# One core of Trainium2: a hybrid pooling, convolution and stick-breaking attention block whose input is normed with tokens on partitions and transposed by TensorE, its projections leaving PSUM unscaled

## The chip, the cores and the metric

The kernel runs on one core of one Trainium2 chip. The metric is the device time in microseconds (us) of one execution, as the median of several runs. The engines are TensorE (PE; its weight loads are listed apart as PEld), VectorE (DVE), ScalarE (ACT), GpSimd (POOL) and SyncE (SP), which here only issues transfers. Each runs its own instructions in order, and instructions on different engines wait for each other through semaphores.

## What is computed

One layer over 1024 tokens of width 1024, all in float32, cut to what matters here:

```
h = x * rsqrt(mean(x*x, -1) + 1e-6) * g_pre                 # pre-norm
u = h @ w_in                       # ten groups of 512 columns, then 3*1024 merge logits
y_pool = pool_mixer(pool_v) * silu(pool_g)
y_conv = gate_b * (causal_conv3(gate_c * conv_x) + bias) * silu(conv_g)
y_sb   = stick_breaking_attention(q, k, v) * silu(sb_g)     # 8 heads of 64
merged = sum over branches of sigmoid(merge_b) * (y_b @ w_branch_b)
out    = x + rms_norm(merged @ w_out, g_post)
```

The norm's factor `rsqrt(...)` belongs to a token, so it may be applied before the projection or after it.

## The kernel before

Everything is held with channels on the partitions and tokens along the free dimension, in two halves of 512 tokens (`HALVES`, t = 0 and 1). Each float32 operand is split into a high part (a cast to float32r) and a low part (operand minus high part), and each product is three matmuls: high by high, high by low, low by high. So one block of 128 output channels of the input projection takes, for each token half, 8 slices of the contraction by 3 matmuls, 24 in all (`half_block`, L136); `block` (L146) runs both halves and hands each PSUM bank to a function `post`.

The host gives x twice: as it is, for the residual at the end, and transposed (`x_t`), with channels on partitions. At the start (L178 to L228) `x_t` comes in seven transfers, in pieces of one to four slices; each slice is multiplied by its channel's `g_pre` and split by ACT (`hh`, L198) and DVE (`hl`, L199), and TensorE takes each slice as it comes. The sum of squares over channels runs beside that: POOL squares (L212, the last four on ACT, L214), DVE adds up (L216), TensorE sums over the partitions (`ssq`, L220), POOL takes the power -0.5 (L133), TensorE spreads the factor over the partitions (`bc`, L224), and DVE copies it to `rstd_bc` (L225). Every projection is then multiplied by `rstd_bc` as it leaves PSUM (`scale_into`, L160 to L163), on DVE.

The first two projected blocks (keys and queries of the first head pair, weights `first_w` and `second_w`) are computed in this start. Then come 64 steps of attention (L395 to L425), one for each head and block of 128 queries: logits `z` (L349, L350) on TensorE, two sigmoids on ACT, a scan on DVE (L354), a product and a mask on POOL (L356, L114), transposes `tp` on TensorE (L373), their split on ACT and DVE (L374, L252), and products `o` with the values (L387). Between these steps TensorE is given projections as filler (`fillers`, L324). A scheduler sets the final order on each engine from the data dependences; the source order is only its start. After the attention come the gates and the branches (`merge_first`, `pool_branch`, `merge_next`, `conv_branch`, `merge_last`) and the output projection with the post-norm.

Weights come through SP's queue in 256 KB pieces, three buffers deep (`next_w`, L82), and are split by ACT (L79) and POOL or DVE (L80).

Of the kernel before, what the change touches and what calls it, by code (L numbers as in the profile page):

```python
# [34 lines left out]
def hybrid_block_kernel(ctx, tc, x, x_t, g_pre, w_in, pool_w, pool_scale, conv_w, conv_b, w_branch, w_out, g_post, out):  # L35
# [16 lines left out]
    bigp = op("big", 2 * KB)  # L52

    def h_tiles(name):
        return [[bigp.tile([P, 2, HALF], F32R, tag="big", name=f"{name}{t}_{i}") for i in range(KB // 2)] for t in range(2)]
# [40 lines left out]
    gpre_sb = const.tile([P, KB], F32, name="gpre_sb")  # L96
    nc.scalar.dma_start(gpre_sb, g_pre)
# [13 lines left out]
    rstd_bc = const.tile([P, S], F32, name="rstd_bc")  # L111
# [17 lines left out]
    def rstd_from(ssq, n, pool):  # L129
        var = pool.tile([P, n], F32, tag="var", name="var")  # L130
        nc.vector.tensor_scalar(out=var, in0=ssq, scalar1=1.0 / D, scalar2=EPS, op0=ALU.mult, op1=ALU.add)
        r = pool.tile([P, n], F32, tag="rstd", name="rstd")
        nc.gpsimd.tensor_tensor(out=r, in0=var, in1=expo[:, 0:n], op=ALU.pow)  # L133
        return r

    def half_block(ps, ws, t):  # L136
        n = 0
        for k in range(KB):
            hi, lo = ws[k // 4]
            a = slice(k % 4 * P, (k % 4 + 1) * P)  # L140
# [37 lines left out]
    with tc.tile_pool(name="xp", bufs=2 * KB) as xp, tc.tile_pool(name="ps_s", bufs=1, space=PSUM) as ps_s:  # L178
        xts, first_w, second_w = [], [], []
        for t, k0, k1 in ((0, 0, 1), (0, 1, 2), (0, 2, 4), (0, 4, 6), (0, 6, 8), (1, 0, 4), (1, 4, 8)):  # L180
            if t == 0 and k0 in (0, 4):
                first_w.append(next_w(0))
            elif k0 == 0:
                q_w = qkp.tile([P, 2, S], F32R, tag="vc", name="q_w", bufs=1)
                hi, lo = q_w[:, 0, :], q_w[:, 1, :]
                for kh, ks in enumerate(HALVES):
                    raw = wraw.tile([P, HALF], F32, tag="raw", name="w_raw")
                    nc.sync.dma_start(raw, w_in[SB_Q, kh])
                    split(raw, hi[:, ks], lo[:, ks], nc.vector)
                    second_w.append((hi[:, ks], lo[:, ks]))  # L190
            xt = xp.tile([P, k1 - k0, HALF], F32, tag=f"xt{t}_{k0}", name="xt", bufs=1)
            nc.sync.dma_start(xt, x_t[t, :, k0:k1, :])
            for k in range(k0, k1):
                xk = xt[:, k - k0, :]
                xts.append(xk)
                gk = gpre_sb[:, k:k + 1]
                hi, lo = hh[t][k // 2][:, k % 2, :], hl[t][k // 2][:, k % 2, :]
                nc.scalar.activation(hi, xk, AF.Copy, scale=gk)  # L198
                nc.vector.scalar_tensor_tensor(out=lo, in0=xk, scalar=gk, in1=f32(hi), op0=ALU.mult, op1=ALU.subtract)  # L199
        banks = [ps_s.tile([P, HALF], F32, tag="first", name="first_ps", bufs=3) for _ in range(3)]  # L200
        banks.append(ps_g.tile([P, HALF], F32, tag="g", name="g_ps"))
        for t in range(2):
            for i, ws in enumerate((first_w, second_w)):
                run(half_block(banks[2 * i + t], ws, t))
        for t in range(2):
            ts = HALVES[t]
            acc = None
            for k in range(KB):
                sq = xp.tile([P, HALF], F32, tag="sq", name="sq", bufs=4)
                xt = xts[KB * t + k]  # L210
                if t == 0 or k < 4:
                    nc.gpsimd.tensor_tensor(out=sq, in0=xt, in1=xt, op=ALU.mult)  # L212
                else:
                    nc.scalar.activation(sq, xt, AF.Square)  # L214
                if acc is not None:
                    nc.vector.tensor_tensor(out=sq, in0=acc, in1=sq, op=ALU.add)  # L216
                acc = sq
            ssq = ps_s.tile([P, 4], F32, tag="ssq", name="ssq")
            for j in range(4):
                nc.tensor.matmul(ssq[:, j:j + 1], acc[:, j * P:(j + 1) * P], ones, start=True, stop=True)  # L220
            r = rstd_from(ssq, 4, xp)
            bc = ps_s.tile([P, HALF], F32, tag="bc", name="bc")
# [465 lines left out]
```

## Time and profile before

| | us |
|---|---|
| median of 3 runs | 1093.85 (1091.54 to 1093.96) |
| the profiled execution's own time | 1091.2 |
| its span, from the first to the last instruction | 1089.5 |
| PE busy in the span | 1055.4 (97%) |
| PEld busy | 871.6 (80%) |
| DVE busy | 484.1 (44%) |
| POOL busy | 413.8 (38%) |
| ACT busy | 367.0 (34%) |

Busy time is an average over stages with different limits, so the table only says that TensorE has little idle time in all. Where it idles, and for whom, is read from the views by stretch, from the waits and from the instructions in order of time.

### The profile page before, as it was taken

Reading aid. Unit: us, or ns where it says so; the run is one execution under the profiler, and the core shown is the slowest. Engines: PE = TensorE matmul, PEld = TensorE weight load, DVE = VectorE, ACT = ScalarE, POOL = GpSimd, SP = SyncE. Lnnn points to the kernel's source line nnn. Section 1 sums busy time; section 2 is a strip of 40 time slices with the busy share of each in tenths; the row PEclk is TensorE's granted clock in tenths of the full one; section 3 lists DMA queues with packets and bytes.
Section 4 is the critical chain, followed back from the end, with each engine's and each line's share of the span. In section 5 each row is a group of like instructions: output and inputs, shape, how many; then the busy total and the mean of one; then the engine's idle time right before and its main releaser. Section 6 shows DMA issues by size and latency. Waiting matters only on the chain.

```text
span 1089.5 us, 12714 instructions
## 1 busy us (share of the span) xinstructions
PE 1055.4 (97%) x4936; PEld 871.6 (80%) x4936; DVE 484.1 (44%) x631; ACT 367.0 (34%) x685; POOL 413.8 (38%) x357
## 2 busy tenths in 40 slices
PE   6889999999999999999999999999999999999997
PEld 4667888878877888888888888888888888888886
DVE  8777777777776111245551111123222311276322
ACT  5367576576655221112221121111111222341111
POOL 5265684676656222221223433342333321440000
PEclk9999999999999999999999999999999999999999
DMA  6001110100100211111111111111111121322311
GB/s 222 30 24 36 29 27 23 40 20 22 38 20 20 68 46 52 49 49 39 43 54 39 55 50 41 49 51 47 51 46 53 56 89 45 114 90 78 116 58 58
DMA packets 29724, 58.25 MB, mean 53 GB/s; under 512 B 3808, under 2 KB 4064, under 8 KB 29408
## 3 DMA queue, kind: packets, MB, share of 16 engines
q1 hardware_dynamic: 29520, 57.43, 17.0%
q8 instruction: 39, 0.64, 0.2%
q14 instruction: 21, 0.17, 0.0%
q10 hardware_dynamic: 144, 0.00, 0.0%
HBM read 53.23 MB, written 4.19 MB: 53 GB/s over the span
## 4 chain that ended last, share of the span: by engine, by line
PE 89%; DVE 4%; ACT 3%; issue 2%; POOL 2%; DMA 1%; SPq 0%; DVEq 0%; POOLq 0%; ACTq 0%
PE g_ps L142 59%; PE pp L448 12%; PE o_ps L592 8%; PE o L387 3%; PE tp L373 3%; PE z L349 1%; PE z L350 1%; ACT khi L265 1%; DVE sq L216 1%; DVE hl L199 1%; DVE sn L354 1%; POOL sp L356 1%; DMA xt<-in_x_t_dram 1%; PE mx L537 1%; DVE wl L252 0%
## 5 line engine op out<-in xcount | busy, mean ns | idle before, releaser
L142 PE MATMUL g_ps<-hh,w_hi 128*128 128x512 f32 x992 | 394.3, 397 | 0.0
L142 PE MATMUL g_ps<-hh,w_lo 128*128 128x512 f32 x992 | 389.8, 393 | 0.0
L142 PE MATMUL g_ps<-hl,w_hi 128*128 128x512 f32 x992 | 388.4, 392 | 0.0
L80 POOL TENSOR_TENSOR w_lo<-w_raw,w_hi 128x512 fp32r<-128x512 f32 x146 | 205.4, 1407 | 427.9 <-ACT w_hi L79 427.9
L142 PEld LDWEIGHTS g_ps<-hh,w_lo 128*128 128x128 f32 x992 | 187.5, 189 | 39.7
L142 PEld LDWEIGHTS g_ps<-hh,w_hi 128*128 128x128 f32 x992 | 187.5, 189 | 35.8
L142 PEld LDWEIGHTS g_ps<-hl,w_hi 128*128 128x128 f32 x992 | 187.4, 189 | 35.2
L79 ACT CAST w_hi<-w_raw 128x512 fp32r<-128x512 f32 x150 | 93.2, 621 | 341.3 <-PE g_ps L142 253.6
L356 POOL TENSOR_TENSOR sp<-sp,sn 128x127 f32<-128x127 f32 (+3 forms) x64 | 85.8, 1341 | 93.3 <-DVE sn L354 52.3
L354 DVE TENSOR_TENSOR_SCAN sn<-sn,masked 128x128 f32<-128x128 f32 (+3 forms) x64 | 105.3, 1646 | 29.2 <-ACT sn L351 26.9
L162 DVE TENSOR_TENSOR gate<-g_ps,rstd_bc 128x512 f32<-128x512 f32 x48 | 33.1, 691 | 185.7 <-PE g_ps L142 185.6
L448 PE MATMUL pp<-yhi,w_lo 128*128 128x512 f32 x192 | 75.9, 395 | 0.0
L448 PE MATMUL pp<-yhi,w_hi 128*128 128x512 f32 x192 | 75.9, 395 | 0.0
L448 PE MATMUL pp<-ylo,w_hi 128*128 128x512 f32 x192 | 75.8, 395 | 0.0
L239 ACT ACTIVATE gate<-gate 128x512 f32<-128x512 f32 x48 | 30.4, 633 | 106.0 <-DVE gate L162 106.0
L162 DVE TENSOR_TENSOR tmp<-g_ps,rstd_bc 128x512 f32<-128x512 f32 x53 | 36.3, 685 | 58.0 <-PE g_ps L142 57.8
L373 PE MATMUL tp<-ident,sp 128*128 128x128 f32 x288 | 45.0, 282 | 15.1 <-DVE wl L252 9.0
L373 PEld LDWEIGHTS tp<-ident,sp 128*128 128x128 f32 x288 | 35.6, 143 | 26.6 <-issue 9.0
L351 ACT ACTIVATE sn<-z 128x384 f32<-128x384 f32 (+2 forms) x96 | 47.5, 494 | 27.5 <-PE z L350 19.8
L252 DVE TENSOR_TENSOR wl<-tp,wh 128x512 fp32r<-128x512 f32 (+2 forms) x96 | 50.4, 545 | 13.9 <-ACT wh L374 12.8
L374 ACT CAST wh<-tp 128x512 fp32r<-128x512 f32 (+2 forms) x96 | 44.3, 487 | 32.5 <-PE tp L373 22.0
L162 DVE TENSOR_TENSOR pb<-g_ps,rstd_bc 128x512 f32<-128x512 f32 x24 | 16.5, 689 | 81.8 <-PE g_ps L142 81.8
(132 smaller groups left out, 1228.3 us busy)
## 6 DMA issues: line engine op xcount, KB each, us to landing
w_raw<-in_w_in_dram SPq DMA_DIRECT2D x128, 256.0 KB, 2.6
w_raw<-in_w_branch_dram SPq DMA_DIRECT2D x24, 256.0 KB, 2.6
wo_raw<-in_w_out_dram SPq DMA_DIRECT2D x16, 256.0 KB, 3.2
xr<-in_x_dram SPq DMA_DIRECT2D x8, 512.0 KB, 4.1
out_dram<-ot SPq DMA_DIRECT2D x15, 256.0 KB, 2.1
xt<-in_x_t_dram SPq DMA_DIRECT2D x2, 1024.0 KB, 10.0
xt<-in_x_t_dram SPq DMA_DIRECT2D x3, 512.0 KB, 7.2
xt<-in_x_t_dram SPq DMA_DIRECT2D x2, 256.0 KB, 4.3
```

Source lines behind the costliest of these rows:

```text
L79: nc.scalar.copy(hi, raw)
L80: eng.tensor_tensor(out=lo, in0=raw, in1=f32(hi), op=ALU.subtract)
L142: nc.tensor.matmul(ps, l[:, a], r[t][k // 2][:, k % 2, :], start=(n == 0), stop=(n == 3 * KB - 1))
L162: nc.vector.tensor_tensor(out=o[:, HALVES[t]], in0=ps, in1=rstd_bc[:, HALVES[t]], op=ALU.mult)
L252: nc.vector.tensor_tensor(out=o, in0=a, in1=f32(b), op=ALU.subtract)
L351: nc.scalar.activation(sn[:, c0:c1], z[:, :w], AF.Sigmoid, scale=-0.125)
L354: nc.vector.tensor_tensor_scan(out=rev, data0=rev, data1=masked[:, S - n:S][:, ::-1], initial=1.0, op0=ALU.mult, op1=ALU.max)
L356: nc.gpsimd.tensor_tensor(out=sp[:, 0:n - 1], in0=sp[:, 0:n - 1], in1=sn[:, 1:n], op=ALU.mult)
L373: nc.tensor.transpose(tp[:, j - j0, :], sp[:, j * P:(j + 1) * P], ident)
L374: nc.scalar.copy(wh[c][:, 0:m, qsub], tp[:, 0:m, :])
L448: nc.tensor.matmul(pp, l[:, a], r[:, HALVES[t]], start=(n == 0), stop=(n == 3 * NB - 1))
L592: nc.tensor.matmul(ps, l[:, a], r[:, es], start=(d == 0 and n == 0), stop=(d == KB - 1 and n == 2))
```

## The change

The transposed input is dropped. x comes in eight transfers of 128 tokens with tokens on partitions (`normed`). For each of them ACT squares and sums along the free dimension (`accum_out`), DVE and POOL make the token's factor, DVE multiplies by the factor and by `g_pre` (now spread over the partitions by a transfer of its own, `g_bc`), TensorE transposes eight 128x128 pieces in two PSUM banks (`xtp`), and ACT and DVE split them out of PSUM into `hh` and `hl`. The sum of squares over partitions, `bc` and `rstd_bc` are gone. A projection leaves PSUM without a factor: as a copy on ACT (token half 0) or DVE (half 1), as a sigmoid by ACT straight from PSUM, or as a product that DVE forms from PSUM with another operand (the SiLU, the convolution's gates). The low parts of the first query weights are made by POOL instead of DVE.

```diff
-    def scale_into(o):
-        def post(t, ps):
-            nc.vector.tensor_tensor(out=o[:, HALVES[t]], in0=ps, in1=rstd_bc[:, HALVES[t]], op=ALU.mult)
-        return post
+    def evict(o, ps, t):
+        if t == 0:
+            nc.scalar.copy(o, ps)
+        else:
+            nc.vector.tensor_copy(o, ps)
+    def copy_into(o):
+        return lambda t, ps: evict(o[:, HALVES[t]], ps, t)
...
+        g_bc = xp.tile([P, D], F32, tag="g", name="g_bc", bufs=1)
+        nc.scalar.dma_start(g_bc, g_pre.broadcast_to([P, D]))
+        def normed(i):
+            xt = xp.tile([P, D], F32, tag="xt", name="xt", bufs=6)
+            nc.sync.dma_start(xt, x[i * P:(i + 1) * P, :])
+            xn = xp.tile([P, D], F32, tag="xn", name="xn", bufs=3)
+            ssq = xp.tile([P, 1], F32, tag="ssq", name="ssq", bufs=4)
+            nc.scalar.activation(xn, xt, AF.Square, accum_out=ssq)
+            var = xp.tile([P, 1], F32, tag="var", name="var", bufs=4)
+            nc.vector.tensor_scalar(out=var, in0=ssq, scalar1=1.0 / D, scalar2=EPS, op0=ALU.mult, op1=ALU.add)
+            r = xp.tile([P, 1], F32, tag="rstd", name="rstd", bufs=4)
+            nc.gpsimd.tensor_tensor(out=r, in0=var, in1=expo[:, 0:1], op=ALU.pow)
+            nc.vector.scalar_tensor_tensor(out=xn, in0=xt, scalar=r, in1=g_bc, op0=ALU.mult, op1=ALU.mult)
+            ts = slice(i % 4 * P, (i % 4 + 1) * P)
+            for kh in range(2):
+                tp = ps_s.tile([P, 4, P], F32, tag="xtp", name="xtp")
+                for j in range(4):
+                    k = 4 * kh + j
+                    nc.tensor.transpose(tp[:, j, :], xn[:, k * P:(k + 1) * P], ident)
+                hi, lo = hh[kh][i // 4][:, :, ts], hl[kh][i // 4][:, :, ts]
+                nc.scalar.copy(hi, tp)
+                nc.vector.tensor_tensor(out=lo, in0=tp, in1=f32(hi), op=ALU.subtract)
+        for i in range(4):
+            normed(i)
+            if i == 1:
+                first_w = [next_w(0), next_w(0)]
...
+        for i, ws in enumerate((first_w, second_w)):
+            for k in half_block(banks[i], ws, 0):
+                if k % 4 == 3:
+                    normed(4 + 2 * i + k // 4)
+        for i, ws in enumerate((first_w, second_w)):
+            run(half_block(banks[2 + i], ws, 1))
...
     def gate_block(g):
-        def post(t, ps):
-            scale_into(g)(t, ps)
-            nc.scalar.activation(g[:, HALVES[t]], g[:, HALVES[t]], AF.Sigmoid)
+        return block(lambda t, ps: nc.scalar.activation(g[:, HALVES[t]], ps, AF.Sigmoid))
+    def silu_block(s):
+        def post(t, ps):
+            nc.scalar.activation(s[:, HALVES[t]], ps, AF.Sigmoid)
+            nc.vector.tensor_tensor(out=s[:, HALVES[t]], in0=ps, in1=s[:, HALVES[t]], op=ALU.mult)
         return block(post)
+    def times_block(o, by):
+        return block(lambda t, ps: nc.vector.tensor_tensor(out=o[:, HALVES[t]], in0=ps, in1=by[:, HALVES[t]], op=ALU.mult))
...
-            run(block(scale_into(z[:, PAD:])))
-            nc.gpsimd.tensor_tensor(out=z[:, PAD:], in0=z[:, PAD:], in1=xc, op=ALU.mult)
+            run(times_block(z[:, PAD:], xc))
...
-            run(block(scale_into(gb)))
-            nc.gpsimd.tensor_tensor(out=acc, in0=gb, in1=acc, op=ALU.mult)
+            run(times_block(acc, acc))
```

The change also moves instructions. At the start, TensorE's first rows before are products; `xn_116`, `xn_140`, `xn_176` and `xn_200` below are the normed tiles of the first four groups of 128 tokens, and `hh0_0`, `hl0_0` the high and low parts of x. TensorE before:

```order
L142 MATMUL first_ps_190<-hh0_0_70,w_hi_125 128x512 [waits Activation_49]
L142 MATMUL first_ps_190<-hl0_0_78,w_hi_125 128x512 [waits DVE_49]
L142 MATMUL first_ps_190<-hh0_0_70,w_lo_126 128x512
L142 MATMUL first_ps_190<-hh0_0_70,w_hi_125 128x512 [waits Activation_49]
L142 MATMUL first_ps_190<-hl0_0_78,w_hi_125 128x512 [waits DVE_49]
```

TensorE now, from its first row:

```order
L193 MATMUL xtp_124<-ident_82,xn_116 128x128 [waits DVE_49]
L193 MATMUL xtp_124<-ident_82,xn_116 128x128 x3
L193 MATMUL xtp_131<-ident_82,xn_116 128x128 x4
L193 MATMUL xtp_148<-ident_82,xn_140 128x128 [waits DVE_49]
L193 MATMUL xtp_148<-ident_82,xn_140 128x128 x3
L193 MATMUL xtp_155<-ident_82,xn_140 128x128 [waits DVE_49,PE_49]
L193 MATMUL xtp_155<-ident_82,xn_140 128x128 x3
```

All 32 transposes of the first four groups now stand ahead of the first product, and each group of four waits until DVE has read an older one out of its bank. DVE at the same place before, from its first work on x:

```order
L199 SCALAR_TENSOR_TENSOR hl0_0_78<-xt_129,gpre_sb_88,hh0_0_70 128x512 [waits DMAHW2_49,DMAHW0_49,Activation_49]
L199 SCALAR_TENSOR_TENSOR hl0_0_78<-xt_133,gpre_sb_88,hh0_0_70 128x512 [waits DMAHW3_49,Activation_49]
L199 SCALAR_TENSOR_TENSOR hl0_1_79<-xt_137,gpre_sb_88,hh0_1_71 128x512 [waits DMAHW4_49,Activation_49]
L199 SCALAR_TENSOR_TENSOR hl0_1_79<-xt_137,gpre_sb_88,hh0_1_71 128x512 [waits Activation_49]
L80 TENSOR_TENSOR w_lo_146<-w_raw_143,w_hi_145 128x512 [waits DMAHW5_49,Activation_49]
```

DVE now:

```order
L80 TENSOR_TENSOR w_lo_165<-w_raw_162,w_hi_164 128x512 [waits DMAHW3_49,Activation_49]
L80 TENSOR_TENSOR w_lo_171<-w_raw_168,w_hi_170 128x512 [waits DMAHW4_49,Activation_49]
L187 SCALAR_TENSOR_TENSOR xn_116<-xt_114,rstd_121,g_bc_112 128x1024 [waits DMAHW1_49,DMAHW0_49,Pool_49]
L187 SCALAR_TENSOR_TENSOR xn_140<-xt_138,rstd_145,g_bc_112 128x1024 [waits DMAHW2_49,Pool_49]
L184 TENSOR_SCALAR var_179<-ssq_177 128x1 [waits Activation_49]
L187 SCALAR_TENSOR_TENSOR xn_176<-xt_174,rstd_181,g_bc_112 128x1024 [waits DMAHW5_49,Pool_49]
L196 TENSOR_TENSOR hl0_0_74<-xtp_124,hh0_0_70 128x4x128 [waits Activation_49]
L184 TENSOR_SCALAR var_203<-ssq_201 128x1 [waits Activation_49]
L187 SCALAR_TENSOR_TENSOR xn_200<-xt_198,rstd_205,g_bc_112 128x1024 [waits DMAHW6_49,PE_49,Pool_49]
L196 TENSOR_TENSOR hl1_0_76<-xtp_131,hh1_0_72 128x4x128 [waits Activation_49]
L196 TENSOR_TENSOR hl0_0_74<-xtp_148,hh0_0_70 128x4x128 [waits Activation_49]
L196 TENSOR_TENSOR hl1_0_76<-xtp_155,hh1_0_72 128x4x128 [waits Activation_49]
```

The split of both first weight pieces now stands ahead of the first normed tile, and the split of a transposed tile stands behind the norm of later ones. The third place is TensorE at the first logits `z` of the attention, where `g_ps` is the value projection. Before:

```order
L142 MATMUL g_ps<-hh_0_70,w_hi 128x512 [waits DVE_49,Activation_49]
L349 MATMUL z<-khi,qa 128x128 [waits DVE_49,PE_49]
L350 MATMUL z<-klo,qa 128x128
L349 MATMUL z<-khi,qa 128x256
L350 MATMUL z<-klo,qa 128x256
L142 MATMUL g_ps<-hl_0_78,w_hi 128x512
L142 MATMUL g_ps<-hh_0_70,w_lo 128x512
L349 MATMUL z<-khi,qa 128x384 [waits Activation_49]
L350 MATMUL z<-klo,qa 128x384
L142 MATMUL g_ps<-hh_0_70,w_hi 128x512
L349 MATMUL z<-khi,qa 128x512 [waits Activation_49]
L350 MATMUL z<-klo,qa 128x512
```

Now:

```order
L343 MATMUL z<-khi,qa 128x128 [waits DVE_49,PE_49]
L344 MATMUL z<-klo,qa 128x128
L343 MATMUL z<-khi,qa 128x256
L344 MATMUL z<-klo,qa 128x256
L132 MATMUL g_ps<-hl_0_76,w_hi 128x512
L132 MATMUL g_ps<-hh_0_72,w_lo 128x512
L132 MATMUL g_ps<-hh_0_72,w_hi 128x512
L132 MATMUL g_ps<-hl_0_76,w_hi 128x512
L132 MATMUL g_ps<-hh_0_72,w_lo 128x512
L132 MATMUL g_ps<-hh_0_72,w_hi 128x512
L132 MATMUL g_ps<-hl_0_76,w_hi 128x512
L132 MATMUL g_ps<-hh_0_72,w_lo 128x512
```

Before, 145 products stood ahead of the first logits (96 of the two first blocks, the whole value block of 48, and one more); now 112 do, and the rest of the value block stands between the logits of the first steps. From the first group of five `tp` transposes on, ahead of which 174 products of the input projection stand in both, TensorE's order is the same in both kernels, instruction by instruction, down to the last.

## Rows read from the trace of the kernel before

**Rows 1.** Busy time by stretch: the stretch (us from the span's start), its length, then for each engine busy time and number of instructions, the granted TensorE clock as a share of full speed, the DMA engines' busy share, GB/s.

```profile
5.25:36.59 31.34, 27.36 (x96) 18.31 (x97) 29.16 (x31) 13.73 (x22) 17.55 (x14) 1.00 0.47 172
36.59:55.45 18.86, 15.70 (x74) 12.80 (x73) 10.91 (x17) 9.71 (x11) 2.04 (x2) 0.91 0.09 28
55.45:74.67 19.22, 15.24 (x72) 11.79 (x72) 14.49 (x19) 12.33 (x32) 13.32 (x14) 0.91 0.11 29
74.67:100.00 25.33, 22.99 (x134) 19.75 (x133) 17.24 (x22) 18.01 (x34) 11.89 (x13) 1.00 0.09 24
100.00:200.00 100.00, 98.00 (x541) 84.22 (x540) 75.69 (x87) 65.49 (x137) 67.50 (x56) 0.98 0.10 29
200.00:300.00 100.00, 97.06 (x541) 82.95 (x540) 74.63 (x92) 66.14 (x143) 63.17 (x55) 0.98 0.11 30
300.00:344.18 44.18, 39.81 (x231) 34.22 (x230) 31.79 (x37) 24.01 (x54) 27.67 (x25) 0.96 0.08 24
344.18:1050.00 705.82, 705.80 (x3090) 579.54 (x3090) 216.50 (x296) 149.69 (x237) 206.34 (x152) 1.00 0.19 58
```

**Rows 2.** Waits of TensorE over the whole span: the waiting line and the one waited for, us in total, times, the longest.

```profile
PE tp L373 <- DVE wl L252: 9.0, 5, 2.3
PE first_ps L142 <- ACT hh L198: 5.6, 2, 5.2
PE first_ps L142 <- DVE hl L199: 3.5, 7, 1.0
PE tp L373 <- POOL sp L114: 3.1, 2, 2.2
PE tp L373 <- POOL sp L356: 2.6, 2, 2.3
```

**Rows 3.** Two pieces of the chain of work that ended last: start, length, what (a count is of instructions back to back).

```profile
201.45 0.87 PE tp L373 x8
...
572.96 10.92 PE g_ps L142 x48
```

**Rows 4.** TensorE in order of time: start, duration, line, what, count; in brackets the idle time before it and what ended it.

```profile
5.25 0.79 PE L142 MATMUL first_ps<-hh,w_hi 128*128 128x512 f32 x1 [5.25 <-ACT hh L198]
...
41.28 0.65 PE L224 MATMUL bc<-ident,rstd 128*128 128x128 f32 x4 [3.16 <-POOL rstd L133]
...
43.40 0.63 PE L142 MATMUL g_ps<-hh,w_hi 128*128 128x512 f32 x1
43.83 0.63 PE L142 MATMUL g_ps<-hl,w_hi 128*128 128x512 f32 x1
...
55.45 0.30 PE L349 MATMUL z<-khi,qa 128*128 128x128 f32 x1
...
64.07 1.05 PE L298 MATMUL tp<-ident,tmp 128*128 128x128 f32 x4
...
74.67 0.71 PE L373 MATMUL tp<-ident,sp 128*128 128x128 f32 x5
```

**Rows 5.** ACT in order of time: three instructions whose wait for a piece of `x_t` shows when that piece had landed.

```profile
4.47 0.72 ACT L198 ACTIVATE hh<-xt,gpre_sb 128x512 fp32r<-128x512 f32 x1 [0.28 <-DMA xt<-in_x_t_dram]
...
8.45 1.33 ACT L198 ACTIVATE hh<-xt,gpre_sb 128x512 fp32r<-128x512 f32 x2 [0.52 <-DMA xt<-in_x_t_dram]
...
15.51 5.11 ACT L198 ACTIVATE hh<-xt,gpre_sb 128x512 fp32r<-128x512 f32 x8 [1.45 <-DMA xt<-in_x_t_dram]
```

**Rows 6.** DMA issues of `x_t`: queue, count, size of each, median us from issue to landing. The pieces are issued small ones first, with 256 KB weight pieces between them.

```profile
xt<-in_x_t_dram SPq DMA_DIRECT2D x2, 1024.0 KB, 10.0
xt<-in_x_t_dram SPq DMA_DIRECT2D x3, 512.0 KB, 7.2
xt<-in_x_t_dram SPq DMA_DIRECT2D x2, 256.0 KB, 4.3
```

**Rows 7.** Groups of instructions by shape over the whole span: line, engine, operation, shapes, count, busy us in total, mean ns of one, idle time before them and what ended it.

```profile
L79 ACT CAST w_hi<-w_raw 128x512 fp32r<-128x512 f32 x150 | 93.2, 621 | 341.3 <-PE g_ps L142 253.6 <-PE pp L448 73.5 <-PE first_ps L142 9.4
...
L162 DVE TENSOR_TENSOR tmp<-g_ps,rstd_bc 128x512 f32<-128x512 f32 x53 | 36.3, 685 | 58.0 <-PE g_ps L142 57.8
...
L252 DVE TENSOR_TENSOR wl<-tp,wh 128x512 fp32r<-128x512 f32 x48 | 32.1, 677 | 5.3 <-ACT wh L374 4.7
...
L374 ACT CAST wh<-tp 128x512 fp32r<-128x512 f32 x48 | 28.0, 592 | 15.6 <-PE tp L373 15.3
...
L502 ACT ACTIVATE sig<-tmp 128x1024 f32<-128x1024 f32 x8 | 8.5, 1061 | 2.4 <-DVE tmp L162 2.4
...
L526 DVE SCALAR_TENSOR_TENSOR pb<-pb,pb 128x1024 f32<-128x1024 f32 x4 | 4.9, 1218 | 0.0
...
L623 POOL TENSOR_TENSOR rstd<-var,expo 128x1 f32<-128x1 f32 x8 | 4.4, 552 | 98.0 <-DVE var L616 98.0
...
L611 ACT ACTIVATION_READ_ACCUMULATOR junk<-o_ps 128x1 f32 x17 | 3.3, 194 | 0.0
...
L225 DVE COPY rstd_bc<-bc 128x512 f32<-128x512 f32 x2 | 1.4, 692 | 3.5 <-PE bc L224 3.5
...
L614 DVE TENSOR_SCALAR var<-ssq 128x1 f32<-128x1 f32 x8 | 1.2, 152 | 33.3 <-ACT junk L611 33.3
```

**Rows 8.** ACT and DVE in order of time where the first keys and queries are split (start, duration, line, what, count).

```profile
47.50 3.18 ACT L265 CAST khi<-tmp 64x1024 fp32r<-64x1024 f32 x3 [8.38 <-DVE tmp L162]
...
54.09 1.22 DVE L252 TENSOR_TENSOR qa<-tmp,qa 64x1024 fp32r<-64x1024 f32 x1
```

More of the change, by code (lines that the diff above doesn't have):

```diff
@@ L51, in hybrid_block_kernel @@
     wsp = op("wsp", 3)
-    bigp = op("big", 2 * KB)
+    bigp = op("big", KB)
     def h_tiles(name):
-        return [[bigp.tile([P, 2, HALF], F32R, tag="big", name=f"{name}{t}_{i}") for i in range(KB // 2)] for t in range(2)]
+        return [[bigp.tile([P, 4, HALF], F32R, tag="big", name=f"{name}{kh}_{t}") for t in range(2)] for kh in range(2)]
     hh, hl = h_tiles("hh"), h_tiles("hl")
@@ L177, in hybrid_block_kernel @@
     first_ops = [tmp_tile(), tmp_tile()]
[L178 to L222, printed above, removed]
-            for j in range(4):
-                nc.tensor.transpose(bc[:, j * P:(j + 1) * P], r[:, j:j + 1].to_broadcast([P, P]), ident)
-            nc.vector.tensor_copy(rstd_bc[:, ts], bc)
@@ new lines, in hybrid_block_kernel @@
+    with tc.tile_pool(name="xp", bufs=2) as xp, tc.tile_pool(name="ps_s", bufs=2, space=PSUM) as ps_s:
+        g_bc = xp.tile([P, D], F32, tag="g", name="g_bc", bufs=1)
[24 more added lines that the diff above has]
+                first_w = [next_w(0), next_w(0)]
+        q_w = qkp.tile([P, 2, S], F32R, tag="vc", name="q_w", bufs=1)
+        second_w = []
+        for kh, ks in enumerate(HALVES):
+            raw = wraw.tile([P, HALF], F32, tag="raw", name="w_raw")
+            nc.sync.dma_start(raw, w_in[SB_Q, kh])
+            split(raw, q_w[:, 0, ks], q_w[:, 1, ks], nc.gpsimd)
+            second_w.append((q_w[:, 0, ks], q_w[:, 1, ks]))
+        banks = [ps_g.tile([P, HALF], F32, tag="g", name="g_ps") for _ in range(3)]
+        banks.append(ps_s.tile([P, HALF], F32, tag="first", name="first_ps", bufs=1))
+        for i, ws in enumerate((first_w, second_w)):
[4 more added lines that the diff above has]
+            run(half_block(banks[2 + i], ws, 1))
@@ L255, in k_block @@
             t = tmp_tile()
-            yield from block(scale_into(t))
+            yield from block(copy_into(t))
             k_parts(p, t)
@@ L272, in q_block @@
             t = tmp_tile()
-            yield from block(scale_into(t))
+            yield from block(copy_into(t))
             q_parts(p, t)
@@ L285, in v_block @@
             t = tmp_tile()
-            yield from block(scale_into(t))
+            yield from block(copy_into(t))
             ops["vt", p] = t
@@ L306, in g_block @@
         def g_block(p):
-            t = tmp_tile()
-            yield from block(scale_into(t))
             s = tmp_tile()
-            nc.scalar.activation(s, t, AF.Sigmoid)
-            nc.vector.tensor_tensor(out=s, in0=t, in1=s, op=ALU.mult)
+            yield from silu_block(s)
             ops["g", p] = s
@@ L498, in silu_of @@
     def silu_of(pool):
-        t = pool.tile([P, S], F32, tag="tmp", name="tmp")
-        run(block(scale_into(t)))
         s = pool.tile([P, S], F32, tag="sig", name="sig")
-        nc.scalar.activation(s, t, AF.Sigmoid)
-        nc.vector.tensor_tensor(out=s, in0=t, in1=s, op=ALU.mult)
+        run(silu_block(s))
         return s
@@ L517, in pool_branch @@
                 nc.vector.memset(b_[:, 0:PAD], 0.0)
-            run(block(scale_into(v[:, PAD:])))
+            run(block(copy_into(v[:, PAD:])))
             sh = 1
@@ L546, in conv_branch @@
             xc = padded(pool, "pb2")[:, PAD:]
-            run(block(scale_into(xc)))
+            run(block(copy_into(xc)))
             z = padded(pool, "pb0")
             nc.vector.memset(z[:, 0:PAD], 0.0)
-            run(block(scale_into(z[:, PAD:])))
-            nc.gpsimd.tensor_tensor(out=z[:, PAD:], in0=z[:, PAD:], in1=xc, op=ALU.mult)
+            run(times_block(z[:, PAD:], xc))
             acc = padded(pool, "pb1")[:, PAD:]
@@ L660 @@
     x = _np.asarray(inputs["x"]).reshape(S, D)
-    v = {"x": x, "x_t": x.T.reshape(KB, P, 2, HALF).transpose(2, 1, 0, 3)}
+    v = {"x": x}
     v.update((name, _np.asarray(inputs[name])) for name in _INS[1:])
     rows = lambda a, n: a.reshape(n, P).T
-    v["pre_norm_g"] = rows(v["pre_norm_g"], KB)
+    v["pre_norm_g"] = v["pre_norm_g"].reshape(1, D)
     nb = v["w_in"].shape[-1] // P
```

20 lines of the change are left out of this document (5 added, 15 removed).

## The prediction

> **What bounds the kernel now.** I read the busy time by stretch first, since the whole-span shares hide where TensorE idles. From 344 us to 1050 us it is busy for 705.80 of 705.82 us at full clock [rows 1]: whatever the change does to DVE, ACT and POOL there (all the gates, the pooling and convolution branches) lies under products and can give nothing back. One product of 128x512 costs 10.92 / 48 = 0.2275 us from start to start, and one 128x128 transpose 0.87 / 8 = 0.109 us [rows 3]; the 394 ns or so that a product is shown busy overlaps the next one.
>
> The idle time of TensorE lies before 344 us, in three kinds. The first product starts at 5.25 us [rows 4], and up to 36.59 us the 96 products of the first two blocks take 31.34 us for 21.8 us of work [rows 1]; they wait for the high and low parts of x, 5.6 us for ACT (5.2 of it the start) and 3.5 us for DVE [rows 2]. Then TensorE waits 3.16 us for the norm's factor [rows 4], and the clock is granted at 0.91 in the two stretches from 36.59 us to 74.67 us [rows 1]: products just after that wait follow each other at 0.43 us, half speed [rows 4]. Around 60 us it waits for POOL's mask and product ahead of the first `tp` transposes, 5.7 us in the whole span [rows 2]. From 74.67 us on, 2.34 + 2.00 + 2.94 + 4.37 = 11.65 us are idle in the attention [rows 1], most of it `tp` waiting for DVE's `wl` (9.0 us in five waits [rows 2]).
>
> The order of TensorE's instructions is the same in both kernels from just before the five `tp` transposes on, which start at 74.67 us before [rows 4]. 174 products stand ahead of them in each. So I compare the time at which each kernel comes to that point, and look apart at whether anything behind it changes.
>
> **The start, step by step.** Before, TensorE could start on any slice of x as it came. Now a product over 512 tokens needs all four groups of 128 tokens normed, transposed and split.
>
> Landing. Before, 0.50 MB (a weight piece and the first piece of x) had landed by 4.47 us, 1.25 MB by 8.45 us and all 4.0 MB by 15.51 us [rows 5, 6], 0.39 MB per us in the second part. Now the 0.5 MB `g_bc` goes out on ACT's queue beside SP's: two groups of x, two weight pieces, two groups, and the query pieces. The second weight piece is 2.0 MB deep with `g_bc` in the line and lands at 10.4 us, or at 9.1 us if `g_bc` costs the line nothing. I take the middle, 9.8 us (an estimate), and keep both ends.
>
> DVE holds both weight splits ahead of the first normed tile. The cast takes 0.62 us and the low part 0.68 us [rows 7], so the first norm (`xn`, 128x1024, 1.22 us [rows 7]) starts at about 11.8 us and the second ends at 14.3 us. The third's factor is asked for only then: variance 0.15 us [rows 7] and handovers, some 0.2 us, the power on POOL 0.55 us [rows 7]; its norm ends at 16.3 us. ACT meanwhile splits the first transposes, casts a query piece (0.62 us) and does the fourth square: 1.06 us and 0.19 us for reading the sum [rows 7]. That square writes a tile that must first be transposed, so it ends only at 16.7 us, and the fourth norm, after variance and power again, ends at 19.0 us.
>
> Only now does DVE split what is left of the first four groups. Two PSUM banks take turns, and a four-piece transpose at low clock takes 1.05 us from first start to last end [rows 4], then ACT's high part 0.59 us and DVE's low part 0.68 us [rows 7]. With the fifth and sixth norms standing between them in DVE's queue (variance, power and norm, 2.0 us each), group 1 is done at 22.2 us, group 2 at 26.2 us, and the first half of group 3 at 28.9 us. Two products need only high parts and may run before; the third waits for 28.9 us.
>
> From there TensorE has 172 products by 0.2275 = 39.1 us, 32 transposes of the other four groups by 0.109 = 3.5 us, and the small ones of the attention's first steps (logits, value and weight transposes, value products). I take these from the stretch 55.45 to 74.67 us: 19.22 us less 29 products (6.6), less idle 3.98, less 1.7 for the clock (0.91 means 18% of it at half speed) = 6.9 us [rows 1]. Sum: 28.9 + 39.1 + 3.5 + 6.9 = 78.4 us.
>
> Two things are added. The first products run at half speed, as those at 43 us did [rows 4]: about 8 of them by 0.20 = 1.6 us (between 0, if the transposes keep the clock up, and 3 us). And some of the later eight groups of four transposes wait for a bank or for ACT's turn; two such waits of 0.5 us, 1.0 us (between 0 and 3). So the point is reached at **81.0 us, against 74.67 us: 6.3 us later**.
>
> The sum has already given the change its gains. The 16 one-column sums, the 8 spreads of the factor and the 3.16 us wait are gone. The first logits don't get earlier by that: keys are split by ACT for 3.18 us and more, and the queries by a cast and DVE's 1.22 us after their last product [rows 8], some 3.3 us in all; 14 products of the value block, 3.2 us, cover it. The other 33 products of that block, ahead of the logits before, now lie between the first logits and the first `tp`, so the waits for POOL around 60 us are covered too.
>
> **The rest of the change.** A copy out of PSUM costs DVE 692 ns where the product with the factor cost 685 ns [rows 7]; what DVE loses is only the half that ACT takes over, at about 0.6 us each. In the dense stage this is worth nothing. In the attention, ACT has 65.49 and DVE 75.69 of 100 us busy [rows 1], so it is a small relief for one and a small load for the other. The long waits there are `tp` behind `wl`, which stands on DVE behind the low parts of keys, and those behind three casts on ACT; none of these moves. I take 0, between a gain of the 11.65 us of idle time with what the clock loses there (0.02 x 100 + 0.02 x 100 + 0.04 x 44 = 5.8 us [rows 1]) and a loss of 3 us. I take the end near 0 because the waiting rows and their order are unchanged.
>
> The page "TensorE: Matmul & The Clock Gate" of the Trainium skill, in "Part 4: PE-mode transpose", gives a 128x128 transpose about 275 ns inside a kernel. By it the 32 transposes behind the first product would take 8.8 us and the sum would be 5.3 us longer; the rows here show eight in 0.87 us [rows 3], so I don't use it. The same section says that transposes don't raise the clock; that agrees with taking the first products at half speed.
>
> Profiled, 1091.2 + 6.3 = 1097.5 us. The median of the runs shown is 1093.85 us, 2.65 us above the profiled execution, so the time that I forecast is **1100.1 us**. A difference of 0.3%, 3.3 us, is about what a measurement of this kernel can tell from no change.
>
> **The rivals.** *The start overlaps better (no change).* If transfers come at the early end and DVE is never held up by an order, four groups cost it 4 x (1.22 + 0.15 + 1.36) = 10.9 us behind the weight splits; with the last power and transposes the third product starts at some 23.5 us, 5.4 us earlier. The difference falls to 0.9 us: 1094.8 us. It decides from 25.9 us on, where less than 3.3 us is left. For it: order and engines are idle enough. Against it: the powers and the fourth square that DVE's queue stands behind. 24%.
>
> *The attention's waits go (faster).* If the lighter DVE and the SiLU without its SBUF-to-SBUF product end the five `wl` waits and the later POOL wait, 9.0 + 2.3 = 11.3 us come back against the 6.3 us lost: 1088.9 us. Against it stands that the instructions ahead of `wl` are the same. It decides once more than 9.6 us are given back. 10%.
>
> *The clock stays low (much slower).* If the second four groups also take some 4 us each, TensorE stops for about 2 us ahead of the second token half and several times before; with the clock at half all the way, 46 products cost 0.20 us more each, 9.2 us, of which 1.6 are in the sum: 6.3 + 7.6 + 2.3 = 16 us, 1110 us. 8%.
>
> That the change fails to do what it says can be left out, since the copies out of PSUM, the transposes and the removed spreads stand in its instruction order.
>
> **How the numbers follow.** My case, 3.3 to 10 us slower, has 58%. Slower by over 0.3% is this and the last rival, 66%; within 0.3% the first, 24%; faster the second, 10%. The range leaves out the faster rival (10%) and the low clock (8%): the lower end takes in the overlapped start with about 2 us of gain in the attention, the upper end the late landing with 3 us each for clock and bank waits: 1092.5 to 1105 us.
>
> **What would show it.** Right: the first `xn` norm near 12 us, the first product that needs a low part between 27 and 31 us, the first logits near 60 us, the five-piece `tp` transposes near 81 us, idle time from there to the end of the attention within 2 us of 11.65 us, and nothing different after it. Wrong: low parts complete by 25 us, `wl` waits well under 9 us, any idle time in the dense stage, or products at half speed past 40 us.

## The result, and the profile after

The changed kernel takes 1096.73 us (median of 7 runs, 1095.61 to 1097.74), the kernel before on the same chip 1092.63 us (7 runs, 1090.64 to 1093.96): a ratio of 1.0034, 95% interval 1.0023 to 1.0046, so 2.5 to 5.0 us slower. The profiled execution took 1095.61 us with a span of 1093.9 us, against 1091.2 and 1089.5 us before: 4.4 us on either count. One kernel's executions differ with their granted clock: the kernel before took 1091.0 to 1092.1 us in ten executions at 0.989 or 0.990 and 1093.3 to 1095.5 us in nine at 0.985 to 0.988 (those beside the first four experiments below), and the profiled execution of the changed kernel has the highest clock of its seven, 0.996. It was forecast 6.3 us slower, at 1097.5 us in the profile and 1100.1 us as a median.

First the start. TensorE in order of time in the changed kernel (start, duration, line, what, count; in brackets the idle time before it and what ended it):

```profile
11.87 1.97 PE L193 MATMUL xtp<-ident,xn 128*128 128x128 f32 x8 [11.87 <-DVE xn L187]
15.68 1.11 PE L193 MATMUL xtp<-ident,xn 128*128 128x128 f32 x4 [1.84 <-DVE var L184]
19.72 1.94 PE L193 MATMUL xtp<-ident,xn 128*128 128x128 f32 x8 [2.92 <-DVE hl L196]
22.21 1.11 PE L193 MATMUL xtp<-ident,xn 128*128 128x128 f32 x4 [0.55 <-DVE hl L196]
25.34 1.97 PE L193 MATMUL xtp<-ident,xn 128*128 128x128 f32 x8 [2.02 <-DVE hl L196]
...
28.60 0.80 PE L132 MATMUL g_ps<-hl,w_hi 128*128 128x512 f32 x1 [0.26 <-DVE hl L196]
...
59.95 0.30 PE L343 MATMUL z<-khi,qa 128*128 128x128 f32 x1 [0.38 <-DVE qa L249]
...
81.53 0.71 PE L367 MATMUL tp<-ident,sp 128*128 128x128 f32 x5
```

The first product that needs a low part stands at 28.60 us, the five `tp` transposes at 81.53 us, where the kernel before had them at 74.67 us [rows 4]: 6.86 us later. Three of the four brackets between 15.68 and 25.34 us name `hl`: transposes wait until a low part has been read out of one of their two banks.

Then the rest. Busy time of the changed kernel by stretch (columns as in [rows 1]), and its waits of TensorE over the whole span (us in total, times, the longest):

```profile
81.53:350.09 268.56, 256.36 (x1441) 219.82 (x1440) 192.48 (x221) 178.22 (x377) 163.39 (x147) 0.99 0.09 28
350.09:1050.00 699.91, 699.89 (x3072) 576.32 (x3071) 172.99 (x234) 151.12 (x253) 187.06 (x144) 1.00 0.19 59
```

```profile
PE tp L367 <- DVE wl L249: 10.7, 6, 2.5
PE xtp L193 <- DVE hl L196: 6.0, 4, 2.9
```

From the five `tp` to the run of projection products that opens the dense stage it takes 268.56 us, where it took 344.18 - 74.67 = 269.51 us [rows 1]. The `wl` waits are not fewer: 10.7 us in six against 9.0 in five [rows 2]. The dense stage is still 100% busy, and yet it is shorter. The chain of work that ended last (start, length, what; a count is of instructions back to back), the kernel before and then the changed one:

```profile
344.18 74.66 PE g_ps L142 x329
418.83 44.80 PE pp L448 x192
...
949.75 44.80 PE pp L448 x192
994.55 86.61 PE o_ps L592 x389
```

```profile
350.09 74.66 PE g_ps L132 x329
424.75 43.96 PE pp L442 x192
...
577.95 10.93 PE g_ps L132 x48
...
954.20 22.00 PE pp L442 x96
976.20 22.24 PE pp L442 x96
998.44 87.30 PE o_ps L580 x390
```

The projections `g_ps` cost the same to 0.01 us (10.93 us for 48, 10.92 before [rows 3]). The branch products `pp`, of the same shape, went from 44.80 / 192 = 0.2333 us each to 43.96 / 192 = 0.2290 us. From the opening run to the first output product `o_ps` the stage takes 998.44 - 350.09 = 648.35 us, where it took 994.55 - 344.18 = 650.37 us: 2.02 us are given back. The output products take 0.69 us more. So 6.86 (start) - 0.95 (attention) - 2.02 (branch products) + 0.69 (output) - 0.18 (what follows) = 4.4 us, the difference of the spans.

### The profile page after: what moved, and what is told of

The parts are those of the page before. It is cut to its first block, busy times and chain, and to the rows that moved or that the text cites. A ratio compares the mean times of both kernels' runs of the same rounds, so it can differ in the third digit from the quotient of the medians.

```text
span 1093.9 us, 12731 instructions
## 1 busy us (share of the span) xinstructions
PE 1053.8 (96%) x4976; PEld 875.5 (80%) x4976; DVE 421.5 (39%) x547; ACT 379.6 (35%) x729; POOL 374.0 (34%) x345
## 4 chain that ended last, share of the span: by engine, by line
PE 89%; DVE 3%; ACT 2%; POOL 1%; issue 1%; POOLq 0%; DVEq 0%; ACTq 0%
PE g_ps L132 60%; PE pp L442 12%; PE o_ps L580 8%; PE o L381 3%; PE tp L367 3%; PE z L343 1%; DVE sn L348 1%; PE z L344 1%; ACT khi L262 1%; DVE klo L249 1%; POOL sp L350 1%; DVE wl L249 1%; PE mx L528 1%; POOL sp L111 0%; ACT sn L345 0%
## 5 line engine op out<-in xcount | busy, mean ns | idle before, releaser
L132 PE MATMUL g_ps<-hh,w_hi 128*128 128x512 f32 x1008 | 400.7, 398 | 0.3 <-ACT hh L195 0.3
L132 PE MATMUL g_ps<-hh,w_lo 128*128 128x512 f32 x1008 | 395.1, 392 | 0.0
L132 PE MATMUL g_ps<-hl,w_hi 128*128 128x512 f32 x1008 | 394.2, 391 | 0.3 <-DVE hl L196 0.3
L80 POOL TENSOR_TENSOR w_lo<-w_raw,w_hi 128x512 fp32r<-128x512 f32 x146 | 194.8, 1335 | 446.0 <-ACT w_hi L79 445.8
L132 PEld LDWEIGHTS g_ps<-hl,w_hi 128*128 128x128 f32 x1008 | 190.2, 189 | 36.6 <-DVE hl L196 1.0
L580 PE MATMUL o_ps<-ohl,mh 128*128 128x512 f32 (+1 forms) x272 | 80.8, 380 | 0.0
L228 ACT ACTIVATE gate<-g_ps 128x512 f32<-128x512 f32 x48 | 28.6, 596 | 89.9 <-PE g_ps L132 89.9
L580 PEld LDWEIGHTS o_ps<-ohl,mh 128*128 128x128 f32 x272 | 49.8, 187 | 11.1
L367 PE MATMUL tp<-ident,sp 128*128 128x128 f32 x288 | 44.6, 282 | 13.5 <-DVE wl L249 10.7
L465 DVE TENSOR_TENSOR gate<-pp,gate 128x512 f32<-128x512 f32 x16 | 11.1, 692 | 117.3 <-PE pp L442 117.3
L580 PE MATMUL o_ps<-ohl,ml 128*128 128x512 f32 (+1 forms) x136 | 51.7, 380 | 0.0
```

The costliest lines, as they stand in the source:

```text
L80: eng.tensor_tensor(out=lo, in0=raw, in1=f32(hi), op=ALU.subtract)
L132: nc.tensor.matmul(ps, l[:, a], r[k // 4][t][:, k % 4, :], start=(n == 0), stop=(n == 3 * KB - 1))
L228: return block(lambda t, ps: nc.scalar.activation(g[:, HALVES[t]], ps, AF.Sigmoid))
L367: nc.tensor.transpose(tp[:, j - j0, :], sp[:, j * P:(j + 1) * P], ident)
L580: nc.tensor.matmul(ps, l[:, a], r[:, es], start=(d == 0 and n == 0), stop=(d == KB - 1 and n == 2))
```

## The experiments

Two questions: is the start really what costs, and by what; and what made the branch products faster. For the second there were two theories. The change makes DVE and POOL lighter (421.5 and 374.0 us busy after, 484.1 and 413.8 before). It also takes `rstd_bc` (4096 bytes a partition) and `gpre_sb` (32 bytes) out of the constant pool, which moves every pool on the left side of SBUF down by 4128 bytes. In a product the weight tile is the stationary operand (128x128, loaded ahead of it) and the tile of 512 tokens the moving one, which streams. In the built programs the first weight tile `w_hi` begins at byte 29888 of a partition before and 25760 after, remainders 64 and 32 by 128; the moving operand `yhi` of `pp` lies on the right side, at 163808 in both, remainder 96. In `g_ps` both operands lie on the left, move together and have equal remainders in every run. In the next four runs theory A is that these addresses made `pp` faster, theory B that the lighter engines did.

**The two halves of the change apart.** In the first run the start is the new one and the rest the old one; in the second the other way round. The first, on the changed kernel:

```diff
+    rstd_bc = const.tile([P, S], F32, name="rstd_bc")
+    nc.gpsimd.memset(rstd_bc, 1.0)
...
-            run(times_block(acc, acc))
+            gb = pool.tile([P, S], F32, tag="tmp", name="tmp")
+            run(block(scale_into(gb)))
+            nc.gpsimd.tensor_tensor(out=acc, in0=gb, in1=acc, op=ALU.mult)
...
```

> The start of the changed kernel (norm, transposes, splits) with the rest of the kernel before: every projection is multiplied on DVE with a tile in place of the factor (filled with ones, since x is already normed), sigmoids read SBUF, POOL makes the two branch products. Nothing of the computation is left out. Theory A (the start costs 6.9 us, and the faster branch products of the dense stage come from where the weight tiles lie in SBUF, not from less work on DVE and POOL): five-piece tp at 81.5 us, 192 branch products in 44.0 us (0.229 us each) as in the changed kernel, since the weight tiles lie as there; the attention gives back nothing or 1 us; in all 4 to 5.5 us slower than before, so within 1 us of the changed kernel. Theory B (the rest's lighter work on DVE and POOL makes these products faster): 44.8 us for 192 (0.2333 us each), 6 to 7 us slower than before.

Measured: ratio 1.0038 (1.0024 to 1.0053), 4.1 us slower than before. The five `tp` come at 81.23 us, and the branch products cost 0.2290 us as in the changed kernel, although DVE and POOL carry the old load:

```profile
426.92 43.96 PE pp L443 x192
```

The weight tiles of this run have the remainder 32, as in the changed kernel. That is theory A, against B. The time is less clear: its interval is 2.6 to 5.8 us, and the profiled execution took 7.1 us more than that of before, 1.5 of them in the attention (271.04 us, at a granted clock of 0.97).

The second run, on the kernel before:

```diff
-            yield from block(scale_into(t))
+            yield from block(copy_into(t))
...
-            run(block(scale_into(gb)))
-            nc.gpsimd.tensor_tensor(out=acc, in0=gb, in1=acc, op=ALU.mult)
+            run(times_block(acc, acc))
...
```

> The start of the kernel before with the rest of the changed kernel: projections leave PSUM unscaled, straight through sigmoids and products. The norm's factor is still computed, but nothing multiplies the later projections by it, so this run leaves the norm out of all but the first two blocks. Theory A: branch products stay at 0.2333 us (192 in 44.8 us), since the weight tiles lie as in the kernel before; the attention gives back 0 to 1 us; in all 0 to 1 us faster than before. Theory B: 192 in 44.0 us and about 1 us in the attention: 2.5 to 3 us faster than before.

Measured: ratio 0.9966 (0.9953 to 0.9980), 2.2 to 5.1 us faster. The branch products did not move, so B falls here too, but the gain is larger than A had it:

```profile
61.39 0.33 PE L385 MATMUL tp<-ident,sp 128*128 128x128 f32 x1 [0.34 <-POOL sp L114]
...
72.66 0.71 PE L385 MATMUL tp<-ident,sp 128*128 128x128 f32 x5
```

```profile
342.19 74.66 PE g_ps L142 x329
416.85 44.80 PE pp L460 x192
```

The five `tp` stand at 72.66 us, 2.0 us before those of [rows 4], and everything after keeps that distance (342.19 - 72.66 = 269.53 us for the attention, 269.51 before). The largest of the waits for POOL's mask around 60 us shrank from 2.2 us [rows 2] to 0.34 us: a weight split that stood on POOL just ahead of that mask now stands elsewhere, as POOL in order of time shows, before and then in this run. What the interval has beyond these 2.0 us goes with the clock: the four of the twelve executions that were granted 0.993 or 0.994 took 1085.95 to 1087.90 us, the other eight, at 0.988 to 0.991, took 1089.26 to 1091.39 us, and the one shown is of these. Under the new start that wait is covered anyway, as the prediction's start sum had it.

```profile
60.02 1.91 POOL L80 TENSOR_TENSOR w_lo<-w_raw,w_hi 128x512 fp32r<-128x512 f32 x1
61.89 1.21 POOL L114 TENSOR_SCALAR_AFFINE_SELECT sp<-sp 128x128 f32<-128x128 f32 x1
```

```profile
60.50 0.83 POOL L114 TENSOR_SCALAR_AFFINE_SELECT sp<-sp 128x128 f32<-128x128 f32 x1
```

**The layout alone.** The same instructions in the same order, with one unused tile. Two runs pad the constant pool by 32 bytes, of the changed kernel and of the kernel before; one pads it by 64 bytes, in the changed kernel; one pads the right side by 32 bytes, in the kernel before. The edits in this order (the first stands for two runs):

```diff
+    pad32 = const.tile([P, 8], F32, name="pad32")
+    nc.gpsimd.memset(pad32, 0.0)
...
+    pad = const.tile([P, 16], F32, name="pad")
+    nc.gpsimd.memset(pad, 0.0)
...
+    rpad = ctx.enter_context(tc.tile_pool(name="rpad", bufs=1, side="right"))
+    pad = rpad.tile([P, 8], F32, name="pad")
+    nc.gpsimd.memset(pad, 0.0)
```

> The changed kernel with one unused tile of 32 bytes a partition in the constant pool, which moves the weight and activation tiles on the left side of SBUF by 32 bytes, so that they stand to the right-side tiles as in the kernel before. Theory A: branch products go back to 0.2333 us (192 in 44.8 us), the output products behind them come 2 us later: 2 us slower than the changed kernel, 6 us slower than before. Theory B: as the changed kernel, 192 in 44.0 us, within 0.5 us of it.

> The kernel before with the same unused 32-byte tile, so that its left-side tiles stand to the right-side ones as in the changed kernel. Theory A: branch products at 0.229 us (192 in 44.0 us), 2 us faster than before. Theory B: as before within 0.5 us, 192 in 44.8 us.

> The changed kernel with one unused tile of 64 bytes a partition in the constant pool. Weight and activation tiles then have the remainder 96 by 128 bytes, as in the kernel before with 32 bytes of padding, and as the normed branch tiles on the right side. Theory A (what a product costs in the dense stage follows from these remainders alone): 192 branch products in 43.5 us, 48 projection products in 10.88 us, output products in 86.6 us, the dense stage 646.2 us long in place of 648.35; 2 to 3 us faster than the changed kernel, 1 to 2 us slower than before. Theory B (only a remainder by 64 counts, and the changed kernel has the better one already): within 0.5 us of the changed kernel.

> The kernel before with an unused 32-byte tile on the right side of SBUF: normed branch tiles and gates there move by 32 bytes to remainder 64 by 128, that of the weight and activation tiles, which stay where they are. Theory A (what counts is whether both operands of a product have the same remainder by 64): 192 branch products in 43.5 to 44 us, projections unchanged at 10.92 us for 48, 2 us or a little more faster than before. Theory C (what counts is the remainder of each operand alone, and 96 is the good one): branch products stay at 44.8 us or get slower.

Measured, as us faster or slower than before from the ratio: changed kernel with 32 bytes 5.4 slower (1.0049, 1.0035 to 1.0064); before with 32 bytes 4.5 faster (0.9959, 0.9943 to 0.9975); changed kernel with 64 bytes 1.2 slower (1.0011, 1.0000 to 1.0023); before with 32 bytes on the right 4.3 faster (0.9961, 0.9945 to 0.9976). Rows of the chain that ended last, in this order:

```profile
352.29 74.66 PE g_ps L134 x329
426.95 44.80 PE pp L444 x192
...
1002.67 86.64 PE o_ps L582 x389
```

```profile
346.54 74.66 PE g_ps L144 x329
421.19 43.52 PE pp L450 x192
...
992.75 86.62 PE o_ps L594 x389
```

```profile
351.83 74.66 PE g_ps L134 x329
426.49 43.52 PE pp L444 x192
...
998.65 86.62 PE o_ps L582 x389
```

```profile
345.70 74.66 PE g_ps L142 x329
420.36 43.52 PE pp L451 x192
...
991.88 86.62 PE o_ps L595 x389
```

By the remainders of `w_hi` and `yhi` by 128:

| runs | `w_hi`, `yhi` | first 192 `pp`, us | one, us |
|---|---|---|---|
| before; old start with new rest; changed + 32 | 64, 96 | 44.80 | 0.2333 |
| changed; new start with old rest; changed with four banks (below) | 32, 96 | 43.96 | 0.2290 |
| before + 32; changed + 64 | 96, 96 | 43.52 | 0.2267 |
| before + 32 on the right | 64, 64 | 43.52 | 0.2267 |

For `pp` theory A holds in every run, and the right-side run rules out that one remainder of `w_hi` is good by itself: 64 was in the slowest pairing, and is as fast as 96 when both operands have it. Equal by 128 is best, 64 apart costs 1%, 32 apart 2.9%. The projections fit: 329 `g_ps` take 74.66 us, 0.2269 us each, in every run shown, with remainders of 64, 32 or 96 that are equal in each. Two details differ from what was expected: before + 32 reached 0.2267 us, not 0.229, since it is equal by 128 and not only by 64; and the dense stage of changed + 64 took 646.82 us where 646.2 was forecast, with 0.4 us of it a wait for a branch tile.

The remainder by 128 is not the whole rule, though. In the changed kernel the tiles of all three kinds of `pp` stand 64 apart, and yet one kind is shown at the 389 ns of equal remainders and one at the 395 ns of tiles 32 apart (line, shapes, count, busy us, mean ns of one):

```profile
L442 PE MATMUL pp<-yhi,w_lo 128*128 128x512 f32 x192 | 75.8, 395 | 0.0
L442 PE MATMUL pp<-yhi,w_hi 128*128 128x512 f32 x192 | 75.3, 392 | 0.0
L442 PE MATMUL pp<-ylo,w_hi 128*128 128x512 f32 x192 | 74.6, 389 | 0.0
```

So 0.2290 us is a mean of the three. The output products show the same. They took 87.30 us in all four runs with the remainder 32 on the left and 86.61 to 86.64 us in all others. In the kernel before, two thirds of them, those with the stationary tile `mh`, have their operands 32 apart, in its two padded versions equal, and there they are shown 2 to 3 ns shorter (392 and 389 ns for 394 and 392); but the third with `ml`, 64 apart in all three, is shown 6 ns longer (398 for 392), and the sum stays at 86.6 us.

The page "SBUF — State Buffer" of the Trainium skill, under "SBUF: two separate sides", gives TensorE a second, independent read port for loading weights beside that of the moving operand. By that alone the pairing of the two addresses would cost nothing; the same products here take 44.80 us in one pairing and 43.52 us in another, so the measurement decides.

**The start.** Four PSUM banks in place of two for the transposes; that is the first pair of lines. A second run has also the statistics first (`stats`: transfer, square, variance and power; `normed` keeps norm, transposes and splits; `xn` has four buffers), and the low parts of the first weights on POOL.

```diff
-                tp = ps_s.tile([P, 4, P], F32, tag="xtp", name="xtp")
+                tp = ps_s.tile([P, 4, P], F32, tag="xtp", name="xtp", bufs=4)
...
-            split(raw, hi, lo, nc.vector if n < 4 else nc.gpsimd)
+            split(raw, hi, lo, nc.gpsimd)
...
-        for i in range(4):
-            normed(i)
+        known = []
+        for i in range(4):
+            known.append(stats(i))
...
+        for i in range(4):
+            normed(i, known[i])
```

> The changed kernel with four PSUM banks in place of two for the transposes of x, nothing else. The scheduler then puts the low parts of groups 1 to 3 ahead of the fifth and sixth norms on DVE. Theory A (the two banks and DVE's queue make the start late, as the prediction's step says): the first product that needs a low part at 22 to 24 us in place of 28.6, the five-piece tp 4 to 6 us earlier, at 76 to 77.5 us; within 1.5 us of before. Theory B (landings, ACT's squares and POOL's powers set the start): not over 1 us earlier than in the changed kernel.

Measured: ratio 0.9973 (0.9963 to 0.9983), 1.9 to 4.0 us faster than before, where within 1.5 us of it was expected. TensorE in order of time, and DVE there in the changed kernel and then in this one:

```profile
11.87 4.47 PE L193 MATMUL xtp<-ident,xn 128*128 128x128 f32 x20 [11.87 <-DVE xn L187]
18.73 2.54 PE L193 MATMUL xtp<-ident,xn 128*128 128x128 f32 x12 [2.39 <-DVE hl L196]
...
22.12 0.54 PE L132 MATMUL g_ps<-hl,w_hi 128*128 128x512 f32 x1
...
73.61 0.71 PE L367 MATMUL tp<-ident,sp 128*128 128x128 f32 x5
```

```profile
23.39 1.28 DVE L187 SCALAR_TENSOR_TENSOR xn<-xt,rstd,g_bc 128x1024 f32<-128x1024 f32 x1 [0.73 <-POOL rstd L186]
24.60 1.28 DVE L196 TENSOR_TENSOR hl<-xtp,hh 128x512 fp32r<-128x512 f32 x2
...
26.66 1.28 DVE L187 SCALAR_TENSOR_TENSOR xn<-xt,rstd,g_bc 128x1024 f32<-128x1024 f32 x1 [0.73 <-POOL rstd L186]
27.86 1.28 DVE L196 TENSOR_TENSOR hl<-xtp,hh 128x512 fp32r<-128x512 f32 x2
```

```profile
17.90 3.87 DVE L196 TENSOR_TENSOR hl<-xtp,hh 128x512 fp32r<-128x512 f32 x6
21.93 0.69 DVE L196 TENSOR_TENSOR hl<-xtp,hh 128x512 fp32r<-128x512 f32 x1 [0.16 <-ACT hh L195]
```

With two banks the last low parts of the first four groups alternate with the fifth and sixth norms, each with a power on POOL (brackets of 0.73 us) in front of it. With four, seven low parts follow each other and the product comes at 22.12 us, 6.5 us earlier; the five `tp` come 7.9 us earlier, 1.1 us ahead of those before the change. Theory A, and more than its 4 to 6 us: in this execution products were back at full speed at 22.50 us, in the changed kernel at 30.40 us. The waits of transposes for `hl` fell from 6.0 to 2.4 us.

> Four banks, and the squares, variances and powers of the first four groups written ahead of their norms (a fourth xn tile), and the low parts of the first weight pieces on POOL in place of DVE. Theory A: the first xn norm at 9 to 9.5 us in place of 10.54, the fourth group's norm 2 us earlier, the first low-part product at 20 to 22 us, the five-piece tp another 1 to 2 us earlier than with four banks alone. Theory B: the weights' low parts (1.2 us or more each on POOL) hold up the powers, or the later groups become late instead: no gain over four banks alone.

Measured: ratio 0.9988 (0.9979 to 0.9997), slower than four banks alone by 0.9 us in the median; theory B, and A missed. The first norm does start at 8.89 us, but the first product that needs a low part only at 23.46 us, because the third power on POOL stands behind the weights' low parts:

```profile
9.01 1.58 POOL L185 TENSOR_TENSOR rstd<-var,expo 128x1 f32<-128x1 f32 x1 [0.88 <-DVE var L183]
10.56 3.49 POOL L80 TENSOR_TENSOR w_lo<-w_raw,w_hi 128x512 fp32r<-128x512 f32 x2
...
14.27 0.55 POOL L185 TENSOR_TENSOR rstd<-var,expo 128x1 f32<-128x1 f32 x1
```

**Both together.** Four banks and the 64-byte tile.

> Four banks for the transposes of x and the 64-byte tile together, on the changed kernel: the two gains should add, since they lie in different stages. Theory A: first low-part product at 22 us, five-piece tp near 73.6 us, 192 branch products in 43.5 us, output products in 86.6 us; 2 to 3 us faster than four banks alone, 5 us faster than before, near 1087.5 us. Theory B (an earlier or denser stretch costs clock or waits elsewhere): less than 1 us faster than four banks alone.

Measured: 1087.21 us, ratio 0.9944 (0.9931 to 0.9958), 4.6 to 7.5 us faster than before and the fastest median of all runs. Low-part product at 22.56 us, five `tp` at 75.23 us; that is 1.6 us later than with four banks alone, with the same instructions. The product itself is 0.44 us later, and in this execution the first products follow each other at 0.43 us, half speed, until 24.69 us, some 1.0 us more. Beside changed + 64, which has two banks and its five `tp` at 81.69 us, four banks give 6.5 us. The layout's gain stands:

```profile
420.80 43.52 PE pp L444 x192
...
992.68 86.62 PE o_ps L582 x389
```

The ratios with and without the tile differ by 0.0029, about 3 us, as theory A had it.

## Why the prediction came out too slow

- **The start: right.** 28.9 us forecast for the first low-part product, 28.60 measured; 81.0 us for the five `tp`, 81.53 measured; 6.3 us later forecast, 6.86 measured. From the one to the other it took 52.9 us, where the sum had 52.1. The first norm was 1.3 us earlier than forecast (10.54 us; ACT cast the two weight pieces back to back from 8.60 us, so the second had landed near the early end of its bounds), which the chain of banks and low parts used up. The half-speed products were about five, not eight. The reason is shown: with four banks the five `tp` come 1.1 us ahead of the kernel before in one profile and 0.6 us behind it in the other, so nearly all of the loss goes. That transposes don't raise the clock, as the prediction took over, fits the changed kernel but not every run: with four banks sixteen transposes followed each other from 11.87 us, the four from 15.68 us took 0.66 us where the changed kernel's four took 1.11 us, and no product had run yet; the clock was then granted at 0.50 from 19.00 to 22.40 us.
- **No long stall around 60 us: right.** The first logits came at 59.95 us, and no wait for POOL stood ahead of the first `tp`.
- **The attention, taken as 0: not shown to differ from it.** The changed kernel's 0.95 us go with the granted clock. From the five `tp` to the dense stage it took 268.56 us at 0.99; 269.51 to 270.14 us at 0.98 (before, old start with new rest, changed with 32 and with 64 bytes); and 270.86 to 271.09 us at 0.97 (the six others), under the old and the new start and rest. Idle time was 12.20 us, as forecast within 2 us of 11.65. What lets the clock fall less often in one execution was not tried.
- **"The dense stage can give nothing back": the step that failed.** It was argued from TensorE being busy 705.80 of 705.82 us. That excludes waits, not a faster or slower product. Its price was 0.2275 us for a product, from one row of `g_ps`; the `pp` of the same shape cost 0.2333 us in the same trace, and no reason was asked. The sign "nothing different after it" failed with it. The removed `rstd_bc` and `gpre_sb` were costed as instructions and not as bytes. Moving the tiles took some 2 us from the branch products (2.02 us in their stage) and went with 0.69 us more on the output. With these two taken back (changed + 32) the loss is 5.4 us (3.8 to 7.0), and the forecast 6.3 us lies in that interval.
- **The offset from profile to median: too large.** 2.65 us, from three runs of before. With seven runs of each, the median of before lies 1.4 us and that of the changed kernel 1.1 us above its profiled execution; both profiles are of executions with a high granted clock (0.991 and 0.996). Of the 3.4 us by which 1100.1 us is too high, 1.9 are the profile's (1097.5 against 1095.61) and 1.5 this offset.
- **The rivals.** Starts overlapping better is what four banks did; with two, the product came well after the 25.9 us from which that rival decides. The attention's waits did not go. The clock was granted at 0.99 in the attention and products were back at full speed at 30.40 us, so the low clock fell too.

## What to carry over

A busy share of 100% says that no wait can be removed, not that products run at their best rate: divide the length of each run of products by its count, and ask why two lines of one shape differ. A change that removes or adds a tile also moves others, so list the SBUF addresses of both operands of the hot products before and after. Equal remainders by 128 were best for the branch products here and gave nothing in the sum of the output products, so try a small unused tile on either side and read each run of products again. In a chain of several engines through a few banks, count the banks first: with too few, the scheduler fills the gap on an engine with later work, which then stands in front.

## What was not expected of the hardware

The rate of the 128x512 float32r branch products depended on how the addresses of their two operands stand to each other: 0.2267 us with equal remainders by 128, 0.2290 us in the mean when 64 apart, 0.2333 us when 32 apart, at a granted clock of 1.00 and with no wait shown inside these runs of products. An unused tile of 32 bytes made the kernel before 4.5 us faster (2.7 to 6.2). Weight loads were shown at 187 to 188 ns in all of these cases and the products at about 389 ns with equal remainders and 395 ns when 32 apart, so it shows in the product's row and not in the load's. Why 32 bytes cost more than 64, and why products 64 apart differ among themselves, stays open.
